# The 16 new sample keys as a zero-filled tile of 128 rows, and score chunks of 512 with a plain rest

## The chip, the core and the metric

The kernel runs on one core of a Trainium2 chip. A core has five engines with queues of their own: TensorE (PE; its weight loads are shown as PEld), VectorE (DVE), ScalarE (ACT), GpSimd (POOL) and SyncE (SP, which here only sends transfers). Each engine works through its instructions in the order in which they stand, and semaphores order the engines among each other. The metric is device time in microseconds (us), the median of several runs, lower being better.

## The reference, cut to what matters

One layer of a streaming encoder is computed for two request groups: a prompt of 2048 rows, and eight running streams ("batches") of 16 new rows each, with 1024 past keys and values per stream. An input projection feeds two branches: a gated spatial mix (branch A) and differential attention with four heads (branch B). An output projection adds the result to the input.

```python
def diff_attend(q, k, v, q_pos, k_pos, lam):
    s = jnp.einsum("bqhcd,bkhcd->bchqk", q, k) * (HEAD_DIM_QK ** -0.5)
    dist = jnp.abs(q_pos[:, None] - k_pos[None, :])
    allowed = (k_pos[None, :] // CHUNK) <= (q_pos[:, None] // CHUNK)
    s = s - alibi_slopes()[None, None, :, None, None] * dist
    s = jnp.where(allowed, s, NEG_INF)
    p = jax.nn.softmax(s, axis=-1)
    a = p[:, 0] - lam * p[:, 1]
    return jnp.einsum("bhqk,bkhd->bqhd", a, v)
...
k_all = jnp.concatenate([past_k, k], axis=1)   # sample: 1024 past keys and 16 new ones
v_all = jnp.concatenate([past_v, v], axis=1)
```

For the prompt a query tile of 128 rows (tile t of 16) sees the keys of tiles 0 to t, so its row of scores is (t + 1) x 128 wide. For a sample stream a row is 1040 wide: eight tiles of 128 keys and a ninth of 16.

## The kernel before

Everything is kept in two float32r parts, a high one (a rounding by ACT, a "cast") and a low one (the rest, by DVE or POOL; `split`, L136). `mm3` multiplies such pairs with three matmuls.

The work is cut into streams, Python generators that yield after a step. `weave` (L877) emits the steps of two streams in a ratio of their times on the tensor engine, and a scheduler below it gives each engine its order: by the order of emission and by when it expects operands to be ready. So a changed instruction moves others, also on other engines. There are these stages:

- The input projection (`acc`) runs alone for the first 190 us or so.
- It then runs beside the sample attention (until about 555 us), and after that beside the prompt attention of query tiles 0 to 7 (until about 945 us). While it runs, products of the projection stand between those of the attention.
- The output projection (`oo`, L1001 on) runs beside the prompt attention of tiles 8 to 15.
- The last tiles of the output projection end the kernel.

**Sample attention.** `sample_scores` (L738) makes the scores of one batch, and `sample_values` (L804) those of the batch before into outputs. The latter goes through nine key tiles `kt`. `load` (L807) fetches a tile of values into `svraw`, ACT casts it to `sv[:, 0]` (L138), and POOL writes the low half `sv[:, 1]` (L139). There are two `sv` buffers, so tile 8's is the one that tile 6's products give back. The weights `a` are transposed into `sa_tp` and split into `saT`, nine slots of two times 64 columns. Then two matmuls for each `kt` add to one bank `sO`, high and low half of the values. For `kt` 8 both operands have `QS` = 16 rows (L808, L828). POOL also adds distances to the scores (`slo`, L784) and works for the projection (`vst`, `xst`, `gb`).

**Prompt attention.** `score_steps` (L548) takes the row of scores of a query tile in chunks. For each chunk and each of the two softmaxes, PE multiplies the keys `kT` by the queries `qT` into a bank `S`, two matmuls for each tile of 512 keys that the chunk touches (L561 to L567). DVE adds the distances, carries the running minimum in `sst` and writes `ex` (L568). After the last chunk ACT takes the exponential (L572). `value_steps` (L592) transposes `ex` into `a_tp` and multiplies it by the values into `oT`. There are two banks `S`. Queries come through `qraw`, one buffer, and a transpose on PE (`q_tp`, L526).

`chunks` (L539) cuts a row of width w into pieces of 512. Where 640 are left it takes 384 and then 256, so that no piece of 128 is left over; the 256 then spans two tiles of keys.

Of the kernel before, what the change touches and what calls it, by code (L numbers as in the profile page):

```python
# [10 lines left out]
F32R = mybir.dt.float32r  # L11
# [4 lines left out]
PSUM = bass.MemoryType.PSUM  # L16
DRAM = bass.MemoryType.DRAM

P = 128
# [4 lines left out]
QS = 16  # L24
# [8 lines left out]
# buffers  # L33
NEX = (4, 2)        # exponentials of the two softmaxes
NW = 12             # weight chunks
NKB = 6             # chunks of transposed keys
NYT = 2             # halves of a transposed row tile of the output projection
XB = 3              # token tiles on the way in
WB = 5              # weight chunks on the way in, at the start
# what the two streams of a stage get of the tensor engine: the first stream's time over the second's, and how many  # L40
# steps of the second the first may run ahead
RS, AS = 2.8, 100   # projection, sample attention
RA, AA = 2.0, 100   # projection, prompt attention
RB, AB = 0.66, 12   # output projection, prompt attention
RT, AT = 1.8, 0     # output projection, last values
LB = 1.5            # factor on RS for the last sample batch
OB, OT = 9, 6       # time of output projection at the head of its two stages
V0, V1 = 0.25, 1.0  # where in a unit of scores the values of the unit before start and end
QP = 0.3            # and where the queries of the unit after are fetched
CA, CB = "dd", "ad" # engine that scales the second softmax of an even and an odd query tile  # L50


def f(ap):
    return ap.bitcast(F32)
# [3 lines left out]
def trunk_step_kernel(  # L58
# [41 lines left out]
    # token tiles: 0..15 prompt, 16 the sample rows  # L100
# [57 lines left out]
    def bank(use, name):  # L158
        """The next of the PSUM banks that the stage gives to this use."""
        turn[use] = turn.get(use, -1) + 1  # L160
        b = cur[use][turn[use] % len(cur[use])]
        return psum.tile([P, 512], F32, name=name, tag=f"bank{b}")
# [5 lines left out]
    class Slots:  # L168
        """A pool of equal slots that the streams of a stage share: a tag takes its slots in turn."""
# [17 lines left out]
    def p1_pools(stage, at):  # L187
# [240 lines left out]
        def stream():  # L428
            """All blocks of columns for the first half of the token tiles and the sample rows, then for the rest."""
# [109 lines left out]
    def chunks(w, m=512):  # L539
        res, x = [], 0  # L540
        while w - x > m:
            step = m - P if w - x == m + P else m
            res.append((x, x + step))
            x += step
        res.append((x, w))
        return res

    def score_steps(sl, dist, h, j, ks, qT, wmax, nex, comb, sm):  # L548
        """A step is one chunk of keys for one of the two softmaxes of a query tile."""
# [97 lines left out]
    def attention(sb, sl, groups, wmax, nk, nv, nex, comb, eng):  # L647
        """A group of pairs of query tiles goes through all heads. The scores of a unit (a pair and a head) run in
        step with the values of the unit before and with the keys and queries of the unit after. Yields None when no
        scores are left."""  # L650
# [28 lines left out]
        for i, (key, j) in enumerate(units):  # L679
            n = size[key[0]]  # L680
            events = []
            # scores
# [5 lines left out]
            # values of the unit before  # L688
# [115 lines left out]
    def sample_values(sa, b, a):  # L804
        bs = slice(b * QS, (b + 1) * QS)

        def load(kt):  # L807
# [3 lines left out]
            v = sa.tile([P, 2, 512], F32R, name="sv", tag="sv")[0:n]  # L811
            split(raw, v[:, 0], v[:, 1], pool)
# [3 lines left out]
        aT = sa.tile([P, 9, 2, 64], F32R, name="saT", tag="saT")  # L816
        for k0, nk, n in ((0, 4, P), (4, 4, P), (8, 1, QS)):
# [9 lines left out]
        for kt in range(9):  # L827
            n = P if kt < 8 else QS  # L828
# [238 lines left out]
```

## Time and profile before

| | |
|---|---|
| median of 3 runs | 1413.92 us (1413.7 to 1422.26) |
| span of the profiled execution | 1410.9 us |
| median less span | 3.0 us |
| mean granted clock of PE | 0.994 |
| instructions | 27990 |
| PE matmuls | 9892 |
| bytes moved by DMA | 183.06 MB, mean 130 GB/s |

The profile is that of one execution. Its span goes from the first to the last instruction; a time around it isn't given for this execution, so the difference to the median of the runs stands for it. A matmul's length in the trace (about 0.28 us for 256 columns, 0.40 for 512) includes its way through the array, and the next one starts before it ends; how long a matmul holds PE is read from one start to the next. In a group, the length goes from the first start to the last end. "Idle" is the time in which an engine had nothing running before a group, with what ended it.

### The profile page before, as it was taken

What the parts mean: (1) busy time and instruction counts of PE and PEld (TensorE: products, weight loads), DVE (VectorE), ACT (ScalarE), POOL (GpSimd) and SP (SyncE); (2) the same over time, 40 slices, a digit from 0 to 9 for tenths busy, and PEclk for the clock granted to TensorE, in tenths of its full rate; (3) what the DMA queues carried; (4) which work ended last, traced back from release to release, by engine and by line L of the source; (5) the groups of instructions that cost most, each with busy time, mean ns of one, the idle gap of its engine ahead of it and who ended that gap; (6) DMA issues with size and microseconds to landing.
All of it is one profiled execution on the core that took longest, in us unless ns stands there. A gap on an engine that the chain in (4) does not pass through costs nothing.

```text
span 1410.9 us, 27990 instructions
## 1 busy us (share of the span) xinstructions
PE 1360.5 (96%) x9892; PEld 1266.1 (90%) x9892; DVE 897.1 (64%) x2114; ACT 794.0 (56%) x1778; POOL 617.6 (44%) x796
## 2 busy tenths in 40 slices
PE   7999999999999989899999999988999999999998
PEld 6999999999999979899999999986888888888887
DVE  5442366767565764786766767444888778878632
ACT  5442356666655775565554655443777767667520
POOL 2361535555554655656232331243555545444310
PEclk9999999999999999999999999998999999999999
DMA  7533244545444476445343332166555433433223
GB/s 220 175 91 100 78 122 124 169 130 158 130 140 145 142 220 203 112 112 138 96 128 83 99 96 69 42 211 207 149 158 162 142 115 117 143 97 94 75 94 101
DMA packets 209245, 183.06 MB, mean 130 GB/s; under 512 B 21104, under 2 KB 167024, under 8 KB 209104
## 3 DMA queue, kind: packets, MB, share of 16 engines
q1 hardware_dynamic: 199280, 155.17, 36.9%
q0 software_dynamic: 9824, 26.09, 6.8%
q8 instruction: 78, 1.28, 0.4%
q14 instruction: 63, 0.52, 0.1%
HBM read 130.86 MB, written 42.47 MB: 123 GB/s over the span
## 4 chain that ended last, share of the span: by engine, by line
PE 50%; DMA 7%; DVE 5%; ACT 3%; issue 3%; POOL 3%; SPq 1%; ACTq 0%; DVEq 0%; POOLq 0%
PE acc L73 16%; PE oo L73 12%; PE S L73 8%; PE oT L73 7%; PE a_tp L77 4%; DMA wraw<-in_w_in_dram 2%; DMA svraw<-in_cache_v_dram 1%; DMA woraw<-in_w_out_dram 1%; DVE ex L584 1%; DMA x<-in_x_prompt_dram 1%; DVE ex L568 1%; PE y_tp L77 1%; DMA qraw<-q_scr 1%; POOL sv L139 1%; DVE w L306 1%
## 5 line engine op out<-in xcount | busy, mean ns | idle before, releaser
L73 PE MATMUL acc<-w,xT 128*128 128x256 f32 x5376 | 719.4, 284 | 2.5 <-DVE w L306 0.9
L73 PEld LDWEIGHTS acc<-w,xT 128*128 128x128 f32 x5376 | 676.2, 190 | 14.8 <-issue 2.7
L73 PE MATMUL oo<-wo,yT 128*128 128x512 f32 x816 | 223.6, 405 | 6.6 <-ACT yT L138 6.6
L73 PE MATMUL S<-kT,qT 128*128 128x512 f32 (+3 forms) x688 | 185.8, 367 | 6.2 <-DVE sst L568 3.9
L572 ACT ACTIVATE ex<-ex,sst 128x128 f32<-128x128 f32 (+15 forms) x128 | 153.9, 1203 | 61.0 <-DVE sst L568 59.5
L73 PEld LDWEIGHTS oo<-wo,yT 128*128 128x128 f32 x816 | 148.9, 191 | 34.7 <-ACT yT L138 7.6
L306 DVE SCALAR_TENSOR_TENSOR w<-wraw,normg,w 128x256 fp32r<-128x256 f32 x224 | 119.6, 555 | 87.1 <-ACT w L305 79.1
L305 ACT ACTIVATE w<-wraw,normg 128x256 fp32r<-128x256 f32 x220 | 105.8, 505 | 87.8 <-DMA wraw<-in_w_in_dram 75.3
L73 PE MATMUL oT<-aT,v 128*128 128x256 f32 x864 | 151.8, 290 | 2.9 <-ACT aT L138 1.9
L568 DVE CUSTOM_DVE_ANT_0 ex<-S,dist,sst 128x512 f32<-128x512 f32 (+2 forms) x192 | 123.2, 652 | 37.6 <-PE S L73 35.8
L73 PEld LDWEIGHTS oT<-aT,v 128*128 128x128 f32 x864 | 124.3, 189 | 14.5 <-DVE aT L139 3.9
L139 POOL TENSOR_TENSOR sv<-svraw,sv 128x512 fp32r<-128x512 f32 (+1 forms) x72 | 96.6, 1346 | 75.5 <-ACT sv L138 59.1
L73 PEld LDWEIGHTS S<-kT,qT 128*128 128x128 f32 x688 | 110.4, 191 | 21.3 <-DVE sst L568 8.6
L138 ACT CAST aT<-a_tp 128x512 fp32r<-128x512 f32 (+1 forms) x144 | 79.3, 559 | 70.4 <-PE a_tp L77 68.5
L139 DVE TENSOR_TENSOR aT<-a_tp,aT 128x512 fp32r<-128x512 f32 (+1 forms) x144 | 94.3, 658 | 38.2 <-ACT aT L138 37.3
L568 DVE CUSTOM_DVE_ANT_0 ex<-S,dist 128x512 f32<-128x512 f32 (+3 forms) x128 | 79.6, 629 | 29.8 <-PE S L73 16.6
L77 PE MATMUL a_tp<-ident,ex 128*128 128x128 f32 x544 | 83.1, 273 | 4.3 <-DVE ex L584 3.3
L784 POOL TENSOR_TENSOR slo<-slo,dist_s 64x256 f32<-64x256 f32 (+1 forms) x64 | 49.4, 772 | 63.3 <-ACT slo L783 60.5
L139 POOL TENSOR_TENSOR v<-vraw,v 128x512 fp32r<-128x512 f32 x36 | 48.2, 1338 | 54.5 <-ACT v L138 45.4
L77 PEld LDWEIGHTS a_tp<-ident,ex 128*128 128x128 f32 x544 | 63.3, 140 | 8.5 <-DVE gbt L641 1.9
L584 DVE SCALAR_TENSOR_TENSOR ex<-ex,sst 128x1024 f32<-128x1024 f32 (+4 forms) x64 | 65.1, 1038 | 1.1
L588 POOL TENSOR_TENSOR ex<-ex 128x1024 f32<-128x1024 f32 (+4 forms) x32 | 58.4, 1848 | 15.9 <-ACT ex L587 11.4
(144 smaller groups left out, 1925.5 us busy)
## 6 DMA issues: line engine op xcount, KB each, us to landing
wraw<-in_w_in_dram SPq DMA_DIRECT2D x160, 128.0 KB, 2.5
skraw<-in_cache_k_dram SPq DMA_DIRECT2D x64, 256.0 KB, 3.1
svraw<-in_cache_v_dram SPq DMA_DIRECT2D x64, 256.0 KB, 2.9
kT<-k_scr POOLq DMA_DIRECT2D x20, 512.0 KB, 4.6
vraw<-out_dram SPq DMA_DIRECT2D x36, 256.0 KB, 2.8
y<-y_scr SPq DMA_DIRECT2D x34, 256.0 KB, 3.0
out_dram<-xo SPq DMA_DIRECT2D x34, 256.0 KB, 2.1
wraw<-in_w_in_dram SPq DMA_DIRECT2D x128, 64.0 KB, 2.2
```

Of the source, the lines that this page charges most:

```text
L73: pe.last = nc.tensor.matmul(*a, **k).ins
L77: pe.last = nc.tensor.transpose(*a, **k).ins
L138: act.copy(hi, src)
L139: (lo_eng or dve).tensor_tensor(out=lo, in0=src, in1=f(hi), op=ALU.subtract)
L305: act.activation(w[:, 0], r, AF.Copy, scale=normg[:, kc:kc + 1])
L306: dve.scalar_tensor_tensor(out=w[:, 1], in0=r, scalar=normg[:, kc:kc + 1], in1=f(w[:, 0]), op0=ALU.mult, op1=ALU.subtract)
L568: dve.tensor_tensor_reduce(out=ex[c][:, a:b], in0=s, in1=dist[:, off + a:off + b], scale=SLOPES[h], scalar=prev[c], op0=ALU.add, op1=ALU.m ...
L572: act.activation(ex[c][:, :w], ex[c][:, :w], AF.Exp, bias=prev[c], scale=-1.0, accum_out=st[:, c, 6:7])
L584: dve.scalar_tensor_tensor(out=p0, in0=p1, scalar=st[:, 1, 7:8], in1=p0, op0=ALU.mult, op1=ALU.add)
L588: pool.tensor_tensor(out=p0, in0=p1, in1=p0, op=ALU.add)
L784: pool.tensor_tensor(out=lo, in0=lo, in1=dist_s[rh, x:x + w_], op=ALU.add)
```

## The change

There are two edits of the code; all else in the diff is comments. In `sample_values` the buffer `sv` of key tile 8 is allocated whole and filled with zeros by POOL before its 16 rows are cast and split into it, `saT[:, 8]` is filled with zeros by POOL, and the matmuls of `kt` 8 take all 128 rows. The zeros add nothing to the sum. In `chunks` the special case for a rest of 640 is gone, so a row is cut into pieces of 512 and a rest of 128, 256 or 384.

```diff
     def chunks(w, m=512):
-        res, x = [], 0
-        while w - x > m:
-            step = m - P if w - x == m + P else m
-            res.append((x, x + step))
-            x += step
-        res.append((x, w))
-        return res
+        return [(x, min(x + m, w)) for x in range(0, w, m)]
...
             n = P if kt < 8 else QS
             raw = sa.tile([P, 512], F32, name="svraw", tag="svraw")[0:n]
             sp.dma_start(raw, cv[b, kt * P:(kt + 1) * P] if kt < 8 else nvs[bs].rearrange("t h d -> t (h d)"))
-            v = sa.tile([P, 2, 512], F32R, name="sv", tag="sv")[0:n]
-            split(raw, v[:, 0], v[:, 1], pool)
+            v = sa.tile([P, 2, 512], F32R, name="sv", tag="sv")
+            if n < P:
+                pool.memset(f(v), 0.0)
+            split(raw, v[0:n, 0], v[0:n, 1], pool)
             return v
...
         aT = sa.tile([P, 9, 2, 64], F32R, name="saT", tag="saT")
+
+        pool.memset(f(aT[:, 8]), 0.0)
...
         for kt in range(9):
-            n = P if kt < 8 else QS
             for i in range(2):
-                pe.matmul(o, lhsT=aT[0:n, kt].rearrange("p s q -> p (s q)"), rhs=vs[kt][:, i],
+                pe.matmul(o, lhsT=aT[:, kt].rearrange("p s q -> p (s q)"), rhs=vs[kt][:, i],
                           start=kt == 0 and i == 0, stop=kt == 8 and i == 1)
```

Over the program, PE has 48 score matmuls less: 48 of 128 columns and 48 of 384 go, 48 of 512 come. POOL has 16 memsets more. ACT and SP have the same instructions, and DVE has 24 chunks each of 512 and 128 where it had 384 and 256. All are laid out in a new order from the first batch on.

On POOL, in the seventh batch (in the trace of before around 509 us), there stood before, from `xst` of a token tile on, the low half of tile 7, the projection's `vst`, and the low half of tile 8 with 16 rows:

```order
L145 TENSOR_SCALAR xst<-xst 128x1
L146 TENSOR_TENSOR xst<-xst,mhalf 128x1
L139 TENSOR_TENSOR sv<-svraw,sv 128x512
L145 TENSOR_SCALAR vst<-vst 128x1
L146 TENSOR_TENSOR vst<-vst,mhalf 128x1
L139 TENSOR_TENSOR sv<-svraw,sv 16x512
```

And POOL at that place now:

```order
L145 TENSOR_SCALAR xst<-xst 128x1
L146 TENSOR_TENSOR xst<-xst,mhalf 128x1
L807 MEMSET sv 128x1024
L139 TENSOR_TENSOR sv<-svraw,sv 128x512
L145 TENSOR_SCALAR vst<-vst 128x1
L146 TENSOR_TENSOR vst<-vst,mhalf 128x1
L139 TENSOR_TENSOR sv<-svraw,sv 16x512
```

The memset for tile 8 stands ahead of the low half of tile 7.

On PE, in the fourth batch (around 379 us before), the rows up to the second product of tile 8 (`sk_tp` are key transposes of the next batch, `sS` its scores) were before:

```order
L73 MATMUL acc<-w,xT 128x256 x6
L77 MATMUL sk_tp<-ident,skraw 128x128 x3
L73 MATMUL sO<-sv,saT 128x512 x2
L77 MATMUL sk_tp<-ident,skraw 128x128
L73 MATMUL acc<-w,xT 128x256 x13
L73 MATMUL sO<-sv,saT 128x512
```

The `x2` is the second product of tile 7 and the first of tile 8. And PE at that place now:

```order
L73 MATMUL acc<-w,xT 128x256 x6
L77 MATMUL sk_tp<-ident,skraw 128x128 x2
L73 MATMUL sO<-sv,saT 128x512
L77 MATMUL sk_tp<-ident,skraw 128x128 x2
L73 MATMUL acc<-w,xT 128x256 x11
L73 MATMUL sO<-sv,saT 128x512
L73 MATMUL acc<-w,xT 128x256 x3
L73 MATMUL sS<-skT,qbd 128x256
L73 MATMUL acc<-w,xT 128x256 x5
L73 MATMUL sS<-skT,qbd 128x256 x3
L77 MATMUL sk_tp<-ident,skraw 128x128
L73 MATMUL acc<-w,xT 128x256 x3
```

The second product of tile 7 and the first of tile 8 now stand apart, with eleven projection matmuls between them, and the second of tile 8 follows behind the last row.

On PE, at the start of the late prompt attention (around 963 to 975 us before), the rows from ahead of the first query transpose to the second (`y_tp` are transposes for the output projection, `k_tp` of keys; the number behind `wo` is a chunk of weights) were before:

```order
L77 MATMUL k_tp<-ident,kraw 128x128 x4
L77 MATMUL y_tp<-ident,y 128x128
L73 MATMUL oo<-wo_11449,yT 128x512
L73 MATMUL oo<-wo_11451,yT 128x512 x3
L73 MATMUL oo<-wo_11453,yT 128x512 x3
L73 MATMUL oo<-wo_11455,yT 128x512 x3
L77 MATMUL q_tp<-ident,qraw 128x128 x2
L73 MATMUL oo<-wo_11440,yT 128x512 x2
L77 MATMUL y_tp<-ident,y 128x128 x4
L73 MATMUL oo<-wo_11440,yT 128x512
L73 MATMUL oo<-wo_11442,yT 128x512 x3
L73 MATMUL S<-kT,qT 128x512 x4
```

Before, three more output products followed these scores, and then the second query transpose. PE at that place now:

```order
L77 MATMUL y_tp<-ident,y 128x128 x4
L77 MATMUL k_tp<-ident,kraw 128x128 x4
L73 MATMUL oo<-wo_11440,yT 128x512 x3
L73 MATMUL oo<-wo_11442,yT 128x512 x3
L77 MATMUL q_tp<-ident,qraw 128x128 x2
L73 MATMUL S<-kT,qT 128x512 x4
L73 MATMUL oo<-wo_11444,yT 128x512 x3
L73 MATMUL S<-kT,qT 128x512 x2
L77 MATMUL q_tp<-ident,qraw 128x128 x2
```

Six output products and a group of `y_tp` have moved from behind the first query transpose to ahead of it, and two score products of the second chunk from behind the second query transpose to ahead of it.

## The prediction

> **What bounds the kernel now.** I read the busy shares first, then the chain that ended last, then the busy time by stretch of the span, and last the matmuls and their neighbours one after the other.
>
> ```profile
> PE 1360.5 (96%) x9892; PEld 1266.1 (90%) x9892; DVE 897.1 (64%) x2114; ACT 794.0 (56%) x1778; POOL 617.6 (44%) x796
> PE 50%; DMA 7%; DVE 5%; ACT 3%; issue 3%; POOL 3%; SPq 1%; ACTq 0%; DVEq 0%; POOLq 0%
> 300.00:400.00 100.00, 99.30 (x792) 95.45 (x791) 63.56 (x147) 60.76 (x158) 55.19 (x65) 1.00 0.46 135
> 945.00:980.00 35.00, 26.68 (x103) 21.02 (x104) 11.18 (x25) 10.39 (x21) 12.69 (x16) 0.80 0.75 233
> 980.00:1345.00 365.00, 356.58 (x2131) 306.34 (x2130) 284.97 (x717) 250.55 (x439) 182.85 (x217) 1.00 0.42 124
> ```
>
> The columns of the last three are the stretch, its length, busy time of PE, its weight loads, DVE, ACT, POOL, then the clock, the DMA share and GB/s. PE is the bound: half of the chain is PE, nothing else has more than 7%. In the middle of the sample stage (300 to 400 us) PE lacks 0.7 us of 100, and POOL, to which the change adds work, is busy for 55. The late prompt attention (980 to 1345) lacks 8.4 us of 365. Only at its start (945 to 980) does PE stand still, 8.3 us of 35, at a clock of 0.80 and a DMA share of 0.75. So time taken off PE in the sample stage or in the scores should show nearly whole at the end, and time put on POOL shows only where PE comes to wait for it.
>
> **Part 1: the product of the 16 new keys takes 128 rows.** Its matmuls keep 512 columns and stay two for each of eight batches. What changes is that their operands have 128 rows in place of 16. Here is what a product with 128 rows (first three lines) and one with 16 (the next three) do to their neighbours; columns are start, length of the group, what it is and how many.
>
> ```profile
> 286.94 1.00 PE L73 MATMUL acc<-w,xTs 128*128 128x256 f32 x7
> 287.78 0.40 PE L73 MATMUL sO<-sv,saT 128*128 128x512 f32 x1
> 288.01 1.23 PE L73 MATMUL acc<-w,xTs 128*128 128x256 f32 x9
> ...
> 425.00 0.61 PE L73 MATMUL acc<-w,xT 128*128 128x256 f32 x3
> 425.53 0.50 PE L73 MATMUL sO<-sv,saT 16*128 16x512 f32 x1
> 425.96 0.62 PE L73 MATMUL acc<-w,xT 128*128 128x256 f32 x3
> ...
> L73 PE MATMUL sO<-sv,saT 16*128 16x512 f32 x16 | 8.2, 510 | 0.0
> ```
>
> With 128 rows: the last of the seven starts at 286.94 + 1.00 - 0.28 = 287.66 (0.28 is one such matmul), 0.12 us before the product; the product holds PE for 0.23 us; the nine behind it follow each other at (1.23 - 0.28)/8 = 0.12. With 16 rows: 425.33 to 425.53 is 0.20 us, the product holds PE for 0.43, and the three behind it take 0.62 where three at 0.12 would take 0.28 + 0.24 = 0.52. That is 0.08 + 0.20 + 0.10 = 0.38 us lost around each, with no wait in front of it (the group's idle time is 0.0 over all 16). If 128 rows cure it, 16 x 0.38 = 6.1 us leave PE. Bounds: nothing, if something other than the row count slows it, and 6.1.
>
> Here the Trainium skill speaks against the change. TensorE: Matmul & The Clock Gate, in LDWEIGHTS (loading the stationary operand), says that a load is set by its columns and not by the contraction rows, and in Why this matters for your kernels that a single small-K matmul takes the time of a full one. For the load the trace agrees (next line: 0.18 us, a full one 0.19). For what surrounds it, the 0.38 us above disagree, so the measurement decides. By the page's rule this part would give nothing, and the sum below would come out 6.1 us higher.
>
> ```profile
> 337.81 0.18 PEld L73 LDWEIGHTS sO<-sv,saT 16*128 16x128 f32 x1
> ```
>
> **Part 2: zeros on POOL.** Eight memsets of 1024 elements for `sv` and eight of 128 for `saT`. Nearest rows of POOL memsets, and three places where they come to stand:
>
> ```profile
> L618 POOL MEMSET aT<- 128x256 f32 x32 | 10.1, 315 | 52.6 <-PE oT L73 50.1 <-DVE sst L568 2.3
> L795 POOL MEMSET sa<- 32x1040 f32 x8 | 7.7, 960 | 3.8 <-PE sa_tp L77 3.1 <-POOLq L1055 0.3
> L724 POOL MEMSET qbd<- 128x640 f32 x1 | 0.6, 632 | 1.1 <-PE x_tp L77 1.1
> ...
> 285.41 1.35 POOL L139 TENSOR_TENSOR sv<-svraw,sv 128x512 fp32r<-128x512 f32 x1
> 288.85 1.28 POOL L139 TENSOR_TENSOR sv<-svraw,sv 16x512 fp32r<-16x512 f32 x1 [2.09 <-ACT sv L138]
> ...
> 379.65 0.73 POOL L394 TENSOR_TENSOR gb<-sg,subg 128x256 f32<-128x256 f32 x1
> 380.34 1.28 POOL L139 TENSOR_TENSOR sv<-svraw,sv 16x512 fp32r<-16x512 f32 x1
> 382.39 0.50 PE L73 MATMUL sO<-sv,saT 16*128 16x512 f32 x1
> ...
> 509.53 0.55 POOL L146 TENSOR_TENSOR xst<-xst,mhalf 128x1 f32<-128x1 f32 x1
> 510.27 1.27 POOL L139 TENSOR_TENSOR sv<-svraw,sv 128x512 fp32r<-128x512 f32 x1 [0.19 <-ACT sv L138]
> 511.60 0.51 PE L73 MATMUL sO<-sv,saT 128*128 128x512 f32 x1 [0.85 <-POOL sv L139]
> ```
>
> From 256 to 640 elements the time grows by (632 - 315)/384 = 0.83 ns an element, so 1024 cost about 0.95 us (960 ns for 1040 agrees) and 128 about 0.21: an estimate from these rows, 9.3 us in all. The `sv` memset adds a wait. It needs the buffer that tile 6's second product frees; behind it on POOL stand the low halves of tiles 7 or 8 and the gates' multiplications, and ACT's cast of the 16 rows waits for it, then PE. Both bounds: nothing where POOL idles, 9.3 us if each stands bare in PE's path. In the second batch POOL sits idle for 2.09 us in just that place (285.41 + 1.35 to 288.85). In the fourth it is busy, and cast and low half of tile 8 would come about 1 us later; but the new order puts the first product of tile 8 eleven projection matmuls (11 x 0.12 = 1.3 us) later, and the second had run 0.8 us after its operand (380.34 + 1.28 to 382.39), with more matmuls ahead of it now. The seventh batch is different: the memset stands ahead of tile 7's low half, behind `xst`. It can start at 510.08 and lasts to 511.03, where the low half had begun at 510.27, and PE was already waiting for that (0.85 us at 511.60). So 0.8 us are exposed there. The `saT` memset is due one batch stage before its tile's last cast and falls into POOL's idle time. I take +0.8 us.
>
> **Part 3: chunks of 512 with a plain rest.** Three query tiles (4, 8, 12) have a width 128 over a multiple of 512: times four heads and two softmaxes, 24 cases. Where 384 + 256 stood, the 256 crossing a key tile, there is 512 + 128. PE had two matmuls of 384 and four of 128 and now has two of 512 and two of 128; columns are equal.
>
> ```profile
> 760.88 1.00 PE L73 MATMUL S<-kT,qT 128*128 128x128 f32 x8
> 761.72 0.45 PE L73 MATMUL acc<-w,xT 128*128 128x256 f32 x2
> ...
> 564.19 0.34 PE L73 MATMUL S<-kT,qT 128*128 128x384 f32 x1
> 1129.07 0.52 PE L73 MATMUL S<-kT,qT 128*128 128x384 f32 x2
> ...
> L568 DVE CUSTOM_DVE_ANT_0 ex<-S,dist,sst 128x512 f32<-128x512 f32 x104 | 76.7, 746 | 21.0 <-PE S L73 19.7
> L568 DVE CUSTOM_DVE_ANT_0 ex<-S,dist,sst 128x384 f32<-128x384 f32 x40 | 24.2, 612 | 8.4 <-PE S L73 8.3
> L568 DVE CUSTOM_DVE_ANT_0 ex<-S,dist,sst 128x256 f32<-128x256 f32 x48 | 22.9, 480 | 8.1 <-PE S L73 7.8
> L568 DVE CUSTOM_DVE_ANT_0 ex<-S,dist 128x128 f32<-128x128 f32 x8 | 2.2, 288 | 1.0 <-PE S L73 0.9
> ```
>
> Eight of 128 hold PE until 761.72, 0.105 us each, which is well above a quarter of the 0.23 that 512 columns take. A 384 takes 0.52 - 0.34 = 0.18. Before: 2 x 0.18 + 4 x 0.105 = 0.78 us a case; after: 2 x 0.23 + 2 x 0.105 = 0.67. That is 0.11 x 24 = 2.6 us less on PE. DVE had 612 + 480 = 1092 ns a case and now has 746 + about 350 (288 and some 60 for the carried minimum) = 1096: nothing. Exponentials, sums and buffers are the same.
>
> **Part 4: what the new order moves.** The scheduler lays all later work out anew. Before the late attention starts, six more output products stand ahead of the first query transpose, so that little is left between it and the next one.
>
> ```profile
> 963.12 0.38 PE L77 MATMUL q_tp<-ident,qraw 128*128 128x128 f32 x2
> ...
> 963.80 0.60 PE L77 MATMUL y_tp<-ident,y 128*128 128x128 f32 x4
> 964.15 1.17 PE L73 MATMUL oo<-wo,yT 128*128 128x512 f32 x4
> ...
> 967.90 1.87 PE L73 MATMUL S<-kT,qT 128*128 128x512 f32 x3 [2.07 <-DVE qT L142]
> 974.34 0.62 PE L77 MATMUL q_tp<-ident,qraw 128*128 128x128 f32 x2 [3.29 <-DMA qraw<-q_scr]
> DMA to landing us min/median/max: 2.2/4.3/9.5
> ```
>
> The second transpose waits for a transfer that can be sent only when the first has given the buffer back, and that landed 9.5 us after its issue; the two stand 11.2 us apart. Before, nine output products, a group of four transposes (963.80 to 964.15) and four score products (9 x 0.23 + 0.35 + 4 x 0.23 = 3.3 us) filled that time, after it six scores and three outputs (9 x 0.23 = 2.1). If the transfer takes as long, 1.3 us more are idle (3.34 - 2.07), since the rest is done earlier and leaves no cover. If it takes the median 4.3, 5.2 us go and the balance is -3.9. I take +1.3: the same queues hold the same transfers there.
>
> **Sum.** -6.1 - 2.6 + 0.8 + 1.3 = -6.6 us. The profiled execution has a span of 1410.9 us; the median of the runs is 1413.92, 3.0 us more, which is what lies around the span, and I let that stand. 1413.9 - 6.6 = 1407.3 us.
>
> **Rivals.** *A, the rows aren't the reason.* The product of tile 8 is slow because its operands come last, by a wait that the profile doesn't show, and zeros don't cure it. Then -2.6 + 0.8 + 1.3 = -0.5, 1413.4 us. For it: this product is always the last of its batch. Against it: idle time 0.0 in front of all 16, and the matmuls behind it are slowed as well. This is also what the Trainium skill's rule above would give.
>
> *B, the other side: the memset takes the product's place on PE's path.* If no POOL idle time covers them, 9.3 us stand where I put 0.8: -6.1 - 2.6 + 9.3 + 1.3 = +1.9, 1415.8 us. It decides as soon as more than 7.4 of the 9.3 us are bare. For it: the seventh batch, and the wait of PE there. Against it: the 2.09 us of idle time in the second, and the later place of the product in the fourth.
>
> *C, the order turns out well.* The query transfer lands in its median time: -6.1 - 2.6 + 0.8 - 3.9 = -11.8, 1402.1 us. For it: the DMA share of 0.75 is a burst that has an end, and the first transpose comes later. Against it: nothing was taken out of the queues.
>
> *D, the order turns out badly.* The late attention's idle 8.4 us double, since its transposes and value products have been moved against the output projection: -6.6 + 8.4 = +1.8, 1415.7 us. For it: PE waits for DVE and ACT results between such groups. Against it: the scheduler spaces them by the same rules.
>
> **Chances.** Forecast 0.66, A 0.11, B 0.09, C 0.07, D 0.07. The forecast alone may miss by some 4 us either way, because waits elsewhere move too. 1402 to 1417 us takes in all four rivals' times and leaves out 0.1 to 0.2. One per cent (14.1 us) is about what a measurement of this kernel can tell from no change. Faster than 1399.8 needs C and more luck in the order: 0.05. Slower than 1428.1 needs B and D together and more: 0.05. Within: 0.90.
>
> **What would show it.** Part 1 is right if `sO` has one form of 128 rows, 144 times, and no product near 0.43 us; it is wrong if the last two of a batch still hold PE that long. Part 2 is right if the memsets read near 950 and 210 ns and PE's waits for POOL's `sv` grow by less than 2 us. Part 3: 640 score matmuls in place of 688, and PE's waits for DVE's minimum unchanged. Part 4: the gap ahead of the second query transpose, near 4.6 us or under 1. The forecast falls if PE's idle time between 190 and 560 us grows by more than the 6.1 us saved, or that after 945 by more than 8.

## The result, and the profile after

| | before | after |
|---|---|---|
| median of 6 runs each | 1418.0 us (1413.7 to 1422.26) | 1425.68 us (1423.07 to 1428.96) |
| ratio | | 1.0065, interval 1.0044 to 1.0086 |
| span of the profiled execution | 1410.9 us | 1426.3 us |
| PE matmuls | 9892 | 9844 |

The changed kernel is slower by 0.65%, some 9 us (0.0065 x 1418 = 9.2), where 6.6 us less were predicted. The two profiled executions lie 15.4 us apart, since that of after is one of its slower runs (1428.19 us) and that of before one of its fastest; sizes taken from the two profiles are therefore somewhat large.

These are the lines of after that answer to those of before: busy shares, the chain that ended last, and three stretches (columns as in the prediction: stretch, length, busy time of PE, weight loads, DVE, ACT, POOL, then clock, DMA share, GB/s).

```profile
PE 1363.9 (96%) x9844; PEld 1266.1 (89%) x9844; DVE 912.1 (64%) x2114; ACT 794.8 (56%) x1778; POOL 629.7 (44%) x812
PE 66%; DMA 9%; DVE 8%; POOL 6%; ACT 5%; issue 5%; SPq 1%; POOLq 0%; DVEq 0%; ACTq 0%
300.00:400.00 100.00, 97.13 (x758) 93.72 (x758) 67.64 (x139) 59.71 (x152) 55.00 (x65) 0.98 0.46 130
945.00:980.00 35.00, 26.11 (x131) 20.86 (x130) 15.46 (x21) 14.09 (x26) 16.93 (x18) 0.90 0.85 276
980.00:1345.00 365.00, 353.22 (x2045) 297.12 (x2046) 285.02 (x718) 248.57 (x436) 182.21 (x216) 0.99 0.44 127
```

The share of PE is the same 96%, and its busy time is 3.4 us more with 48 matmuls fewer. In the middle of the sample stage it gets through 758 matmuls in 100 us where it got through 792. In the late attention it lacks 11.8 us of 365 (365 - 353.22) where it lacked 8.4, and gets through 2045 where it got through 2131; the output projection starts 7.1 us later in this profile (955.1 against 948.0), so the two windows don't hold quite the same work. The two chains can't be compared share by share: that of before, whose shares add up to 72%, is followed back only to 409 us, that of after to the start.

**Where the time went.** To compare stretches of equal work I counted instructions on PE: "sample" is the time from the 1501st to the 3301st projection matmul, "late" that from the second to the 816th output product. (The expectations below say "from the first to the 3300th"; their numbers are those of "sample".) In the two profiles the start brings 2.4 us, sample 7.6 (345.4 to 353.0), the middle -2.9, late 7.9 (458.1 to 466.0), and the end 0.4: together 15.4.

**The product of tile 8** has 128 rows now. Here are its two of the third batch, from the timeline of PE after, and its group:

```profile
348.41 1.22 PE L73 MATMUL acc<-w,xT 128*128 128x256 f32 x9
349.47 0.40 PE L73 MATMUL sO<-sv,saT 128*128 128x512 f32 x1
349.70 0.52 PE L73 MATMUL acc<-w,xT 128*128 128x256 f32 x3
...
L73 PE MATMUL sO<-sv,saT 128*128 128x512 f32 x144 | 53.1, 414 | 6.5 <-ACT sv L138 4.0 <-POOL sv L139 2.3
```

The last of nine starts at 348.41 + 1.22 - 0.28 = 349.35, 0.12 us before the product, which holds PE for 0.23, and three follow in 0.52: just like any other. So the 0.38 us are gone. But the idle time in front of these products has become 6.5 us, from 2.8.

**The second batch** shows what came instead. From the timeline of after, by engine: ACT, POOL, DVE, PE.

```profile
289.59 2.35 ACT L793 ACTIVATE sa<-sp,sst 32x1040 f32<-32x1040 f32 x2
...
292.38 1.31 ACT L305 ACTIVATE w<-wraw,normg 128x256 fp32r<-128x256 f32 x3
293.59 0.60 ACT L138 CAST sv<-svraw 16x512 fp32r<-16x512 f32 x1
...
290.89 0.96 POOL L807 MEMSET sv<- 128x1024 f32 x1
294.27 2.59 POOL L139 TENSOR_TENSOR sv<-svraw,sv 16x512 fp32r<-16x512 f32 x2 [2.43 <-ACT sv L138]
...
293.64 3.51 DVE L306 SCALAR_TENSOR_TENSOR w<-wraw,normg,w 128x256 fp32r<-128x256 f32 x3
297.07 0.41 DVE L378 SCALAR_TENSOR_TENSOR usg<-sg,acc 128x256 f32<-128x256 f32 x1
...
294.25 0.50 PE L73 MATMUL sO<-sv,saT 128*128 128x512 f32 x1 [0.61 <-ACT sv L138]
294.88 0.39 PE L73 MATMUL sS<-skT,qbd 128*128 128x256 f32 x1
297.63 2.69 PE L73 MATMUL acc<-w,xT 128*128 128x256 f32 x12 [2.36 <-DVE usg L378]
```

And before, ACT, DVE and PE (POOL's low half of the 16 rows was the row at 288.85 in the prediction):

```profile
288.16 0.60 ACT L138 CAST sv<-svraw 16x512 fp32r<-16x512 f32 x1
...
289.87 1.16 ACT L799 ACTIVATE sa<-sp,sst 32x1040 f32<-32x1040 f32 x1
...
289.48 0.93 DVE L306 SCALAR_TENSOR_TENSOR w<-wraw,normg,w 128x256 fp32r<-128x256 f32 x1
290.33 0.41 DVE L378 SCALAR_TENSOR_TENSOR usg<-sg,acc 128x256 f32<-128x256 f32 x1
290.67 0.47 DVE L306 SCALAR_TENSOR_TENSOR w<-wraw,normg,w 128x256 fp32r<-128x256 f32 x1
...
290.80 0.49 PE L73 MATMUL sO<-sv,saT 16*128 16x512 f32 x1
```

The cast of the 16 rows had stood ahead of the exponentials `sa`. The scheduler, which now knows of a memset before it, has put it behind both exponentials and three casts of weights. The buffer is free when tile 6's second product ends, at 290.15 (289.75 + 0.40), and the cast starts at 293.59: 3.4 us later, where it had been 1.3 (286.87 to 288.16). Some 0.7 of the 3.4 go by on POOL, which does tile 7's low half first (that tile's cast has moved behind a long exponential too, and runs at 288.96 where before it ran at 284.65), 0.96 are the memset, which ends at 291.85, and 1.7 the order on ACT. So the low half of the 16 rows comes late and back to back with that of the next batch's tile: 2.59 us on POOL without a pause. Beside them DVE's three `w` take 3.51 us, where one takes 0.47 (row at 290.67). `usg`, queued behind them, is late, the bank of PSUM that it reads isn't freed, and the projection stands still for 2.36 us. The memset's own time, which I had expected to be hidden here, is the smaller part of the delay; the order around it is the larger.

**The late attention.** First the query transposes that the prediction spoke of, then a gap that wasn't there before (DVE, then PE):

```profile
972.84 0.44 PE L77 MATMUL q_tp<-ident,qraw 128*128 128x128 f32 x2 [1.04 <-DMA qraw<-q_scr]
...
982.57 0.66 PE L77 MATMUL q_tp<-ident,qraw 128*128 128x128 f32 x2 [4.60 <-DMA qraw<-q_scr]
...
1290.76 2.47 DVE L578 SCALAR_TENSOR_TENSOR ex<-ex,sst 128x1024 f32<-128x1024 f32 x2
1293.15 0.69 DVE L139 TENSOR_TENSOR yT<-y_tp,yT 128x512 fp32r<-128x512 f32 x1
...
1290.90 0.98 PE L73 MATMUL oT<-aT,v 128*128 128x256 f32 x6
1293.94 0.63 PE L77 MATMUL y_tp<-ident,y 128*128 128x128 f32 x4 [2.06 <-issue]
```

At 1290.76 DVE combines the two softmaxes (2.47 us) ahead of the low half of `yT`; the next `y_tp` starts 0.1 us after that low half, and behind six value products nothing else stands on PE in between. Before, the same combination had output products beside it:

```profile
1284.04 2.48 DVE L584 SCALAR_TENSOR_TENSOR ex<-ex,sst 128x1024 f32<-128x1024 f32 x2
...
1284.08 2.55 PE L73 MATMUL oo<-wo,yT 128*128 128x512 f32 x10
```

### The profile page after: what moved, and what is told of

Its sections match the earlier page's. It is cut to its first block, busy times and chain, and to the rows that moved or that the text cites. A ratio compares the mean times of both kernels' runs of the same rounds, so it can differ in the third digit from the quotient of the medians.

```text
span 1426.3 us, 27915 instructions
## 1 busy us (share of the span) xinstructions
PE 1363.9 (96%) x9844; PEld 1266.1 (89%) x9844; DVE 912.1 (64%) x2114; ACT 794.8 (56%) x1778; POOL 629.7 (44%) x812
## 4 chain that ended last, share of the span: by engine, by line
PE 66%; DMA 9%; DVE 8%; POOL 6%; ACT 5%; issue 5%; SPq 1%; POOLq 0%; DVEq 0%; ACTq 0%
PE acc L73 32%; PE oo L73 11%; PE S L73 7%; PE oT L73 6%; PE a_tp L77 4%; DMA wraw<-in_w_in_dram 3%; DMA svraw<-in_cache_v_dram 2%; DVE ex L562 1%; DVE w L306 1%; PE sS L73 1%; POOL sv L139 1%; DMA x<-in_x_prompt_dram 1%; DMA qraw<-q_scr 1%; PE sk_tp L77 1%; DMA woraw<-in_w_out_dram 1%
## 5 line engine op out<-in xcount | busy, mean ns | idle before, releaser
L306 DVE SCALAR_TENSOR_TENSOR w<-wraw,normg,w 128x256 fp32r<-128x256 f32 x224 | 126.9, 587 | 81.0 <-ACT w L305 72.1
L73 PEld LDWEIGHTS S<-kT,qT 128*128 128x128 f32 x640 | 104.4, 190 | 28.5 <-DVE sst L562 17.0
L578 DVE SCALAR_TENSOR_TENSOR ex<-ex,sst 128x1024 f32<-128x1024 f32 (+4 forms) x64 | 68.4, 1090 | 1.1
L573 POOL TENSOR_SCALAR sst<-sst 128x1 f32<-128x1 f32 x64 | 20.8, 325 | 106.0 <-ACT ex L566 102.9
```

Source lines behind the costliest of these rows:

```text
L73: pe.last = nc.tensor.matmul(*a, **k).ins
L306: dve.scalar_tensor_tensor(out=w[:, 1], in0=r, scalar=normg[:, kc:kc + 1], in1=f(w[:, 0]), op0=ALU.mult, op1=ALU.subtract)
L573: pool.tensor_scalar(out=st[:, 0, 7:8], in0=s0, scalar1=s0, scalar2=EPS, op0=ALU.mult, op1=ALU.mult)
L578: dve.scalar_tensor_tensor(out=p0, in0=p1, scalar=st[:, 1, 7:8], in1=p0, op0=ALU.mult, op1=ALU.add)
```

## The experiments

All were timed in five rounds beside runs of the kernel before on the same chip; a ratio is to those. The table has the two stretches of each profile, in us, and what the order of PE's instructions is in the late stretch: P, Q and R are names for orders that several kernels share (in Q, one query transpose of e8 and e14 stands two score products later than in e1 and e3), "own" is one that no other kernel here has.

| kernel | sample | late | late order | ratio and interval |
|---|---|---|---|---|
| before | 345.4 | 458.1 | P | |
| after | 353.0 | 466.0 | own, R from the 341st product on but for a few moved before the 511th | 1.0065 (1.0044 to 1.0086) |
| e1 zeros and 128 rows, old chunks | 353.8 | 469.2 | Q | 1.0101 (1.0082 to 1.0121) |
| e2 plain chunks alone | 345.4 | 466.6 | R | 1.0055 (1.0033 to 1.0076) |
| e3 zeros, 16 rows, old chunks | 355.2 | 470.5 | Q | 1.0105 (1.0081 to 1.0128) |
| e4 128 rows, no memset in the batch, old chunks | 346.2 | 456.7 | P | 0.9990 (0.9973 to 1.0006) |
| e5 as e4, plain chunks | 346.5 | 467.2 | R | 1.0019 (1.0005 to 1.0034) |
| e6 before, another late order | 349.5 | 471.5 | own | 1.0085 (1.0061 to 1.0109) |
| e7 as e2, another late order | 345.8 | 471.3 | own | 1.0074 (1.0052 to 1.0096) |
| e8 as e1, `sv` filled by DVE | 353.4 | 471.2 | Q | 1.0111 (1.0086 to 1.0137) |
| e9 as e3, zeros beside the 16 rows | 346.0 | 459.9 | P | 0.9998 (0.9984 to 1.0012) |
| e10 before, another sample order | 359.4 | 464.1 | P but for its start | 1.0048 (1.0032 to 1.0065) |
| e11 as e5, another late order | 348.9 | 477.4 | own | 1.0092 (1.0067 to 1.0116) |
| e12 as e5, another late order | 348.5 | 477.6 | own | 1.0083 (1.0065 to 1.0101) |
| e13 as e3, memset of 16 columns | 349.9 | 458.5 | P | 1.0053 (1.0034 to 1.0072) |
| e14 before, with the late order of e1 | 347.6 | 471.5 | Q | 1.0077 (1.0057 to 1.0096) |

How far a profile can be trusted is seen from kernels with the same order: before, e2, e6 and e7 have one order up to the middle stage, and their sample stretch takes 345.4, 345.4, 349.5 and 345.8 us. After and e1 share another order there, and take 353.0 and 353.8. So 350 can't be told from 345 there, 353 and more can.

Part of that spread is the clock. The time in the sample stretch for which PE's granted clock was 0.50 is 3.4 us in before, e5, e7, e9 and e13, 6.8 in e11, e12 and e14, 10.2 in after, e1, e2, e4 and e10, 13.7 in e8, 17.1 in e3 and e6. With like compared with like, the kernels with zeros lose 7.6 and 8.4 us in after and e1 (against e2), 5.7 in e3 (against e6), 4.5 in e13 and 0.6 in e9 (both against before).

**The parts alone: e1, e2, e3.** e1 is the padding without the chunks, e2 the chunks without the padding. e3 takes the memsets but leaves the product at 16 rows:

```diff
-            v = sa.tile([P, 2, 512], F32R, name="sv", tag="sv")[0:n]
-            split(raw, v[:, 0], v[:, 1], pool)
+            v = sa.tile([P, 2, 512], F32R, name="sv", tag="sv")
+            if n < P:
+                pool.memset(f(v), 0.0)
+            split(raw, v[0:n, 0], v[0:n, 1], pool)
...
+        pool.memset(f(aT[:, 8]), 0.0)
...
-                pe.matmul(o, lhsT=aT[0:n, kt].rearrange("p s q -> p (s q)"), rhs=vs[kt][:, i],
+                pe.matmul(o, lhsT=aT[0:n, kt].rearrange("p s q -> p (s q)"), rhs=vs[kt][0:n, i],
```

> The zero-filled tile alone, chunks as before. Theory Z (the zeros cost more than they save): the 16 products give back 6.1 us, the memsets' waits and their hold on the two engines take some 10, so +3 to +6 us against the kernel before (ratio 1.002 to 1.004). Theory C (the chunks cost): 5 us faster, 0.996. Theory O (any new order lands within some us, here by chance on the bad side): either, within 6 us.

> The plain chunks alone, 16-row products as before. Theory Z: 2 us faster by the two matmuls saved in each of 24 cases, ratio 0.998. Theory C (a chunk of 512 in place of 384 keeps a score bank longer, and PE waits for DVE's minimum): +4 us or more, 1.003 or more, with PE's waits for the minimum near 10 us in place of 6. Theory O: either way by a few us.

> The memsets stay, but the last product takes 16 rows as before, and chunks are as before: cost without gain. Theory Z: +9 to +12 us, ratio 1.006 to 1.008. Theory C: +1 us, the memsets being hidden. Theory O: anything within 6 us of before.

Each part alone is slower than before, e1 and e3 by more than any of their expectations had. e3 loses as much as e1, so the zeros cost and the rows don't pay for them. e2 loses nothing in the sample stage and 8.5 us late; its ratio is the one that Theory C asked for, but PE's waits for DVE's minimum are 6.2 us, not near 10.

**128 rows without a memset in the batch: e4, e5.** `saT` is one buffer whose slot 8 is filled once; the 16 rows go into the buffer of tile 6, whose other rows hold old values, and these meet zeros in `saT`.

```diff
-            v = sa.tile([P, 2, 512], F32R, name="sv", tag="sv")[0:n]
+            if kt < 8:
+                v = sa.tile([P, 2, 512], F32R, name="sv", tag="sv")
+            else:
+                v = vs[6]
+                sa.turn["sv"] += 1
...
```

> The product takes 128 rows without a memset per batch: the weights' ninth slot is zeroed once for all batches, and the 16 new values are written over the first rows of key tile 6's buffer, whose other rows then meet zero weights; chunks as before. Theory Z: the whole 6 us show, 1412 where before has 1418, ratio 0.996. Theory C: the same as the zero-filled tile alone, within 1 us. Theory O: anything within 6 us of before less 6.

> 128 rows without a memset per batch (as in the run before, which came out level with the kernel of before) and the plain chunks. Theory C (the chunks themselves cost): 7 us slower than that run, so about 1.005 of before. Theory O (the chunks cost by the new order alone): another order, so anything from 0.994 to 1.006, and other waits in the late attention than the plain chunks alone had.

e4 loses nothing: the sample stretch is back at 346.2, and the late one, in exactly the order of before, at 456.7. It doesn't win the 6 us of Part 1 either. By the usual distance of each matmul from the one before it, as the profile of before has it, PE's own work in the sample stretch fell from 314.6 to 309.9 us, but what comes on top of it (waits, and matmuls at half clock) rose from 30.8 to 36.2. e5 adds the chunks, begins the output projection 5.3 us earlier than before did (942.7 against 948.0; why its middle stage is shorter isn't shown), and ends 3.6 us later. Its ratio lies in Theory O's range and below Theory C's 1.005, but its late stretch, 467.2, is that of e2.

**Order alone, late: e6, e7.** One constant of the planner, the share that the output projection gets, is changed; no instruction is added or removed.

```diff
-RB, AB = 0.66, 12
+RB, AB = 0.67, 12
```

> The kernel of before with the late attention's ratio at 0.67 in place of 0.66: every instruction as before, those after the start of the output projection in another order, no change ahead of that. Theory C: within 2 us of before, ratio 0.999 to 1.001. Theory O: the part behind the start of the output projection moves by 3 us or more, most likely upwards, since the order of before was tuned.

> The plain chunks alone with that ratio at 0.67, so the same work as the plain chunks alone in another order. Theory C: as the plain chunks alone, 1.0055 of before within 0.001. Theory O: more than 3 us off that, either way.

e6 does the work of before, in its order up to the output projection, and loses 13.4 us behind that. e7's late stretch is 4.7 us longer than e2's, but its ratio is only 0.0019 above e2's (2.7 us), and the intervals overlap: by the ratio it decides nothing.

**The engine that writes the zeros: e8.** The memset of `sv` is DVE's (`dve.memset(f(v), 0.0)`), the rest as in e1.

> The zero-filled tile alone (chunks as before), its eight large memsets on DVE in place of POOL. Theory W (the cast of the 16 rows waits for the memset): the sample stage still ends 8 us or more late, like the run with POOL's memsets. Theory P (the memset pushes POOL's low halves together, and these hold DVE up): the sample stage loses less than 3 us.

Sample takes 353.4 us against 353.8, so taking the zeros off POOL doesn't bring the time back. But that isn't yet Theory W: PE's longest waits in this stretch are now for DVE's `w` (2.6 us) and `sa` (2.1), on the engine that spends 7.3 us on the zeros, and the gap at `usg` in the second batch is gone. So e8 doesn't clear POOL's time.

**The wait, and the order that follows from it: e9, e10.** e9 is e3 with its zeros written only to the upper 64 partitions of the same buffers, where nothing reads them; a memset takes as long there (952 ns against 957), but in six of eight batches the cast no longer has to wait for it. The diff is against e3. e10 is before with `RS` at 2.82 in place of 2.8.

```diff
-                pool.memset(f(v), 0.0)
+                pool.memset(f(v[64:P]), 0.0)
...
-        pool.memset(f(aT[:, 8]), 0.0)
+        pool.memset(f(aT[64:P, 8]), 0.0)
```

> The zeros of e3 with the same size on POOL, but written to partitions 64 to 127 of the same buffers, which nothing reads; the product keeps 16 rows, the chunks are the old ones. In six of eight batches ACT's cast of the 16 rows no longer waits for the memset; POOL's work is that of e3. Theory W (the cast's wait on the memset costs the time in the sample stage): the stretch from the first to the 3300th projection matmul falls from e3's 355 us to 345 to 350 us, as in the kernel before (345). Theory P (POOL's occupied time and the low halves behind it cost it): it stays at 352 to 356 us. The late part's order is not quite that of before: by the theory that every other order of it costs 8 us or more the ratio is 1.005 to 1.010; if it stays near 1.000, a late order near that of before is good enough.

> The kernel before with the projection's share of the sample stage at 2.82 in place of 2.8: the same instructions in another order from the sample stage on, late part included. If the sample stage's loss in the changed kernel (345 to 353 us from the first to the 3300th projection matmul) came of another order alone, it shows here too, with 350 us or more; if it came of the zeros, this stage stays at 345 to 350 us. By the theory that the late order of before is a favourable one, the late part (from the second output product to the 816th) takes 465 to 472 us where it took 458, and the ratio is 1.005 to 1.010; otherwise within 0.003 of 1.

e9 has e3's memsets, and its sample stretch is 346.0 where e3's is 355.2 (some 4 us of that difference are clock, by e6 against before). In its second batch (ACT, then POOL) the cast stands ahead of the exponentials again, and the low half of the 16 rows runs by itself:

```profile
287.88 0.61 ACT L138 CAST sv<-svraw 16x512 fp32r<-16x512 f32 x1
...
289.32 2.35 ACT L799 ACTIVATE sa<-sp,sst 32x1040 f32<-32x1040 f32 x2
...
286.83 0.95 POOL L813 MEMSET sv<- 64x1024 f32 x1 [0.52 <-PE sO L73]
288.57 1.29 POOL L139 TENSOR_TENSOR sv<-svraw,sv 16x512 fp32r<-16x512 f32 x1 [0.78 <-ACT sv L138]
```

e10 shows that an order can cost this stage more than the zeros do: 359.4 us with not one instruction more. By the test set for it, that speaks for a loss by the order alone; e9 against e3 shows that the zeros' wait is what brings such an order here. Its late part is P but for the first hundred output products, and only these are slow: from the 477th on it takes 139.1 us, as in before, e4 and e9.

**More late orders for 128 rows and plain chunks: e11, e12.** `RB` is 0.65 and 0.68 in the kernel of e5.

> e5 (128 rows without a memset for each batch, plain chunks) with the output projection's share of the late stage at 0.65 in place of 0.66: the same instructions in another late order. Theory O (the late order decides): the late part lies anywhere from 456 to 472 us, the ratio from 0.994 to 1.009, and nothing before 945 us changes. If plain chunks themselves cost (theory C), the late part stays at 465 us or more.

> As the run before with a share of 0.68: one more late order of the same instructions. Theory O: the late part differs from that at 0.65 and 0.66 by some us in either direction, within 456 to 472 us. Theory C: 465 us or more in all three.

Both came out above the upper end of the expectation (472 us), 10 us above e5. So the late order does decide, by more than I had put. But 465 or more in all three is also what Theory C had: the five orders seen with plain chunks (with that of after) all lay at 466 and above. Whether the chunks themselves cost there, or another order with them would reach 458, stays open.

**The wait without the work: e13; the late order of e1 without its zeros: e14.** e13 is e3 with a memset of 16 columns (`f(v[:, 0, 0:16])`), 0.12 us on POOL. e14 is before with `RS` at 2.78, which happens to give the late order of e1, e3 and e8.

> As e3 (zeros, 16-row product, old chunks), but the memset of sv covers 16 of its 1024 columns, so that ACT's cast of the 16 rows still waits for it while POOL has next to nothing to do. The order of the sample stage is near that of e3, the order from there on is that of the kernel before. Theory W (the wait, with the order that follows from it, costs the sample stage 8 us): the stretch from the first to the 3300th projection matmul takes 352 to 356 us, the late part 457 to 460, the ratio 1.005 to 1.007. Theory P (the 0.95 us on POOL cost it): that stretch takes 345 to 350 us, and the ratio is within 0.002 of 1.

> The kernel before with the projection's share of the sample stage at 2.78 in place of 2.8: no instruction more or less, another order in the sample and middle stages, and from the output projection on the order of e1, e3 and e8. Theory O (the late loss of those three is their order alone): the late part, from the second output product to the 816th, takes 468 to 472 us, as in them (469.2, 470.5, 471.2), where the kernel before took 458. If their zeros or an earlier delay carried it there, it takes 457 to 462 us. The sample stage may lie anywhere from 345 to 360 us.

In e13 the second batch goes as in the changed kernel (POOL, DVE, PE):

```profile
288.65 0.12 POOL L813 MEMSET sv<- 128x16 f32 x1
291.64 2.59 POOL L139 TENSOR_TENSOR sv<-svraw,sv 16x512 fp32r<-16x512 f32 x2 [2.87 <-ACT sv L138]
...
291.42 3.10 DVE L306 SCALAR_TENSOR_TENSOR w<-wraw,normg,w 128x256 fp32r<-128x256 f32 x2
294.44 0.41 DVE L378 SCALAR_TENSOR_TENSOR usg<-sg,acc 128x256 f32<-128x256 f32 x1
...
295.00 2.06 PE L73 MATMUL acc<-w,xT 128*128 128x256 f32 x16 [2.81 <-DVE usg L378]
```

So that gap needs the wait and its order, not the microsecond of zeros. For the whole stage the two readings differ: the profile (its fastest run) has 349.9, between the two theories, while the timed runs have 1.0053, what the wait alone was expected to cost; e9, whose later order is the same, has 0.9998. Part of this is the clock: the profiled run had a mean granted clock of 0.994, the other five 0.986 to 0.991, and before beside them 0.993 in the mean. At like clock e13 loses 4.5 us and e3 5.7, so I take the wait, with the order that it brings, for the larger part, and leave open how much POOL's time adds.

e14 lies at 471.5 us late, inside 468 to 472. It has the gaps of e1 in the same places; here is one of them on PE, first from e1, then from e14:

```profile
1159.51 0.61 PE L77 MATMUL a_tp<-ident,ex 128*128 128x128 f32 x4
1161.89 0.63 PE L77 MATMUL k_tp<-ident,kraw 128*128 128x128 f32 x4 [1.77 <-issue]
```

```profile
1154.34 0.61 PE L77 MATMUL a_tp<-ident,ex 128*128 128x128 f32 x4
1156.73 0.63 PE L77 MATMUL k_tp<-ident,kraw 128*128 128x128 f32 x4 [1.78 <-issue]
```

Over all kernels the late stretch takes 456.7 to 459.9 us in order P (four kernels), 466.6 and 467.2 in R, 469.2 to 471.5 in Q (four), whatever was done before it. That the late loss is one of order alone is shown for Q, by e14, and for the order of e6. The changed kernel's order is nearly R from the 341st output product on, which e2 has without the padding: from the 477th on after takes 145.4 us, e2 144.0, and P 139.1. The gap of after at 1293.94 stands there in e2 too:

```profile
1283.10 0.98 PE L73 MATMUL oT<-aT,v 128*128 128x256 f32 x6
1286.13 0.63 PE L77 MATMUL y_tp<-ident,y 128*128 128x128 f32 x4 [2.06 <-issue]
```

For the first part of its late order no kernel was run that has it without the padding.

What an order costs isn't all waiting. In the late stretch PE idles for 15.1 us before, 19.1 after and 21.2 in e6, and its clock is 0.50 for 12.2, 14.6 and 22.7 us; if each microsecond of the latter costs half of one, some 5 of e6's 13.4 us are clock (an estimate from these figures). The timed runs say the same: the mean granted clock was 0.986 to 0.988 in the four kernels of order Q, and 0.992 or 0.993 in before, after, e2, e4, e5 and e9. Of the runs of before beside the experiments, the 24 at 0.994 or more had a median of 1412.1 us, the 17 at 0.990 or less one of 1415.9. Why some orders have the lower clock, no run here shows.

No version beat both kernels: e4 is level with before.

## Why the prediction was wrong

- **Part 1 (-6.1): the cause was right, the yield wrong.** The 16 rows were what slowed the product; with 128 it reads 0.12, 0.23 and 0.12 us. Rival A falls. (The rule of the Trainium skill, TensorE: Matmul & The Clock Gate, by which this part would give nothing, is not borne out for what surrounds the product.) But I booked time taken off PE in this stage as time off the end, because PE lacked only 0.7 us of 100 there. That share hid the slack: by the usual distances 30.8 of the stretch's 345.4 us were already more than PE's work. In e4, which has this part alone, nearly all of the 4.7 us that came off the work went back into such time: 0.9990 is 1.4 us, with an interval from 3.8 us less to 0.8 more. Time put on PE needn't show there either: e2, in before's order, had 6.8 us more at half clock and took the same 345.4 (e6, with 13.7 more, took 349.5). What else holds that stretch isn't shown.
- **Part 2 (+0.8): the term that failed, 6 to 8 us in its place** (353.0 to 355.2 us in after, e1, e3 and e8 where e4 and e9 take 346; at like clock 5.7 to 8.4). The memsets' own times were right, as their two groups in after show:

```profile
L807 POOL MEMSET sv<- 128x1024 f32 x8 | 7.7, 957 | 2.1 <-PE sO L73 2.1
L814 POOL MEMSET saT<- 128x128 f32 x8 | 1.6, 206 | 6.6 <-PE sO L73 6.5
```

  So was the seventh batch: PE's wait for tile 7's low half grew from 0.85 to 1.96 us. What I did was to lay the memset into POOL's idle time at the place where the second batch had it, with every other instruction where it had stood. The wait I had named, ACT's cast behind the memset, I priced as a delay of that cast alone. The scheduler answered it by another order on POOL and ACT, so that in the second batch the cast came 3.4 us after its buffer was free where it had come after 1.3, and the low half met `w` on DVE. The mark I had set for this part, that PE's waits for POOL's `sv` grow by less than 2 us, even held: they went from 1.5 to 2.3. The loss went to waits for others too (2.7 + 2.3 + 2.4 us more for ACT's `sv`, DVE's `skT` and `usg`, against 0.8 for POOL's `sv`), as the waits of PE in the sample stage show, after (208 to 564 us) and then before (208 to 555):

```profile
PE sO L73 <- ACT sv L138: 4.0, 6, 1.6
PE sS L73 <- DVE skT L139: 3.0, 3, 1.4
PE acc L73 <- DVE usg L378: 2.4, 1, 2.4
PE sO L73 <- POOL sv L139: 2.3, 3, 2.0
```

```profile
PE sO L73 <- POOL sv L139: 1.5, 3, 0.8
...
PE sO L73 <- ACT sv L138: 1.3, 3, 0.5
...
PE sS L73 <- DVE skT L139: 0.7, 2, 0.5
```

- **Part 3 (-2.6): right on PE, worth nothing at the end.** By the usual distances PE's work behind the sample stage fell from 783.2 to 780.1 us. With the chunks comes another late order in every kernel that has them, and a late stretch that is some 8 us longer or more. The mark that PE's waits for DVE's minimum stay unchanged didn't hold: 3.9 us before, 6.5 after, 6.2 in e2. It doesn't single out the chunks, since e1 and e6, with the old ones in other orders, have 6.8 and 6.9. So it stays open whether the chunks themselves cost late or only the orders that came with them.
- **Part 4 (+1.3): right at the place I looked at, wrong as the whole.** The second query transpose waits for its transfer for 4.60 us, near the 4.6 forecast. With the waits between the two, PE lost 1.04 + 4.60 us to `qraw` and 1.4 to `qT` where it had lost 3.3 and 2.1: 1.6 more. But the new order ran on for another 400 us, and I priced one place of it. The late stretch grew by 7.9.
- **The rivals.** B and D together come near the +9.2 measured: -6.6 + 8.5 + 8.4 = +10.3. That is partly luck. By B the sample stage would have lost 9.3 - 6.1 = 3.2 us, where the profiles have 7.6, and its mechanism was wrong, since the zeros' time on POOL was, in the second batch and by e13, the smaller part of what came to stand on PE's path. D I gave 0.07 with the remark that the scheduler spaces such groups by the same rules. That was the weak step: of the late orders that were run here, every one but that of before cost 6 us or more (those with plain chunks with the doubt named under Part 3). I treated the order of before as one of many alike, and it was the best that was seen.
- **The signs.** I had said that the forecast falls if PE's idle time between 190 and 560 us grows by more than 6.1 us, or that after 945 by more than 8. The first came true: 9.7 us before, 17.2 after. The second went from 21.9 to 27.4, by 5.5. The 1% that I took for what a measurement can tell from no change was too coarse: the interval of the ratio is 0.2% either way.

## What to carry to other kernels

Where a scheduler lays a program out anew, an edit that is local in the code is priced in two parts: the edited instructions, and a new order for all that follows, whose spread is measured by re-laying the same instructions (a constant of the planner moved by 0.7 to 1.5% was enough here, and gave +0.48 to +0.85%). If that spread is larger than the edit's gain, find a form of the edit that leaves the order as it is, as e4 does with one buffer written once, before judging the edit. And a new wait is priced by what the scheduler moves because of it, seen in the order, not by the idle time of the engine that does the added work.

## What the hardware showed unexpectedly

A product with 16 contraction rows between products of 128 costs PE 0.38 us more than one with 128, and zeros cure it. It isn't one place: in the trace of before 15 of the 16 products hold PE for 0.42 or 0.43 us (the sixteenth, at half clock, for 0.66), where one with 128 rows takes 0.23.

DVE's `w`, which reads two operands in SBUF, is held while POOL runs an operation with two tensor inputs, but not while POOL fills zeros. The rows at 293.64 and 294.27 above show 3.51 us for three (the third alone runs from 294.44 to 297.15, through both of POOL's operations); beside a memset three take 1.27 (DVE, then POOL, after):

```profile
550.43 1.27 DVE L306 SCALAR_TENSOR_TENSOR w<-wraw,normg,w 128x256 fp32r<-128x256 f32 x3
...
550.65 0.96 POOL L807 MEMSET sv<- 128x1024 f32 x1 [2.05 <-PE sO L73]
```

The Trainium skill, SBUF — State Buffer, in SBUF: two separate sides, says that the two engines share a pair of ports, held for a whole instruction, and that a DVE operation with two SBUF inputs contends only with a POOL operation that reads SBUF. The trace agrees with both halves.

After the gap at 294.9 PE's clock fell to half for 3.4 us, which it did not do between 200 and 510 us before. Here is a stretch of that time (columns as above; the clock is the third figure from the end):

```profile
298.00:300.00 2.00, 2.00 (x11) 2.00 (x11) 1.47 (x4) 0.51 (x1) 0.00 (x0) 0.50 1.00 343
```

In e13 a longer wait at the same place (2.81 us against 2.36) left the clock whole. In e1 and e3, with the same gap of 2.36 us, it was at half for 6.8. So such a gap may cost another 1.7 to 3.4 us (half of 3.4 and of 6.8) or nothing, and it can't be told beforehand from the length of the gap.
